# Halves after the next chunk's decays, decayed queries on VectorE, masks inside the clamp

## The chip, the cores and the metric

The kernel runs on one core of a Trainium2 chip. The metric is the device time of one execution in microseconds (us), the median of several runs. The engines are named as the profile names them: PE is TensorE (matmuls, with PEld for its weight loads), DVE is VectorE, ACT is ScalarE, POOL is GpSimd, SP is SyncE, whose queue issues all DMAs of this kernel. PE has two clock levels, 2.4 and 1.2 GHz; the profile gives the granted clock as a share of the higher one.

## The reference, cut to what matters

The model has two layers (1024 channels, 256 context tokens and 256 latent tokens). Each layer is a half-step feed-forward part, a token mixer and another feed-forward part. The token mixer runs three recurrences over the tokens in both directions and merges them: a gated delta rule (4 heads), retention (4 heads) and Mamba-2 SSD (16 heads in 2 groups). The last layer gives an output for the latent tokens alone.

The delta rule, in chunks, needs per head and direction a triangular matrix of key products with decays, and a matrix of query-key products with decays:

```python
diff = gc[..., :, None] - gc[..., None, :]
a_mat = (einsum('nbhik,nbhjk->nbhij', kc, kc)
         * where(strict, exp(where(strict, diff, 0.0)), 0.0) * bc[..., :, None])
sol = triangular_solve(eye(CHUNK) + a_mat, rhs, left_side=True, lower=True)
p_mat = (einsum('nbhik,nbhjk->nbhij', qc, kc)
         * where(incl, exp(where(incl, diff, 0.0)), 0.0))
```

The SSD scan (chunk_gla) has the same decays, and its part from the state is the query, decayed, times the state:

```python
intra = einsum('nbghij,nbghjv->nbghiv', scores[:, :, :, None] * dmat, vc)
o_c = einsum('bgik,bghkv->bghiv', xc[3], s) * xc[4][..., None]     # q s, times q_dec = exp(gc)
oc = (oc_f + flip(oc_b) + D * sx) * silu(s_z)
yc = rms_norm(oc per group, ssd_norm_g)
```

## The kernel before

All matmuls of weights are done as three passes of a split number: a value is cast to a shorter float (its high half) and the rest is the low half; L141 to L143 (mm3) multiply high by high, high by low and low by high. Each weight block (128x512) is loaded by SP's queue (raw, L110), cast on ACT (whi, L121) and subtracted on DVE or POOL (wlo, L123; pool_lo says which blocks go to POOL). Four blocks can be ahead of PE.

Every instruction is written in a program order, and a planner (the framework's scheduler, with its own costs) sets from that order and from what is ready in its model the order of each engine's queue. Queues then run strictly in that order. DMAs are in SP's queue, weight loads and others mixed.

The mixer (mix_main, L1424) runs the delta rule (gdn, L781) and lets a generator fill PE beside it: self.take(us) draws so many microseconds of projections (gdn_z, retention, ssd_project) from it. In layer 0 gdn runs twice with two heads and four output chunks of 128 tokens (och = 0 to 3); in layer 1 once with four heads, in two pairs, with output for chunks 2 and 3 alone. The preparation, L889 to L937, does for each pair of heads and each chunk c:

- L905: clamps on DVE. Rg holds the running sums of log decays as rows (loaded from DRAM by rows_in), G the same as columns. Slots 0 and 1 of E are min(Rg - G, 0) forward, slots 2 and 3 the same backward (only for output chunks), slots 4 and 5 are max(Rg - G, 0) backward. L908 and L909 take exp on ACT.
- L912, L915: key-key and key-query products on PE, into PSUM (ps).
- L917: kks, the key products times the strict upper mask triUs, on DVE. L920 and L921: M = kks * column * E. L923: M times the rows Rb on POOL.
- L928: kq = key-query products * column * mask (triU or triL), four on DVE. L930: PT = kq * E.
- L936, L937: the decayed queries Q of the delta rule (ACT, POOL).

Then the 32x32 diagonal blocks of M go to DRAM and back (L945, L952: d1, B), a substitution on DVE inverts them in 31 steps (L957, L959), merges of blocks make the inverse of the chunk, and the scan over chunks follows.

The SSD part (ssd, L1219) runs after the delta rule, per group g of 8 heads, with the merge (gates and branch projections) as PE's filling. prep(c, d) makes for chunk c and direction d the decays: Relu and exp on ACT (L1281, L1283) for E; and where a state comes in (c != d) exp of the rows R (L1287), times the queries BC (L1288: POOL in layer 0, DVE in layer 1). out(c) does the products (L1314), the gating (L1317), the mean of squares (L1319, L1323), the reciprocal root in eight small DVE instructions on 128x1 (tile snv, L1326, then rsqrt, L252 to L260), its broadcast by PE (L1330), the scaling (L1333), and last the halves of the chunk (L1336 cast on ACT to ysch, L1337 subtract on DVE to yscl), which the third branch of the merge reads. The loop at L1349 runs prep(next, 0), out(c), prep(next, 1).

Of the kernel before, what the change touches and what calls it, by code (L numbers as in the profile page):

```python
# [8 lines left out]
F32 = mybir.dt.float32  # L9
# [6 lines left out]
P = 128  # L16
# [30 lines left out]
class Net:  # L47
# [410 lines left out]

    def mix_setup(self, ctx):
        nc, io, cp = self.nc, self.io, self.cp  # L460
        self.masks = cp.tile([P, 3, P], F32, name="masks")
        nc.sync.dma_start(out=self.masks, in_=io["masks"])
        self.triU, self.triL, self.triUs = (self.masks[:, i, :] for i in range(3))
        self.prow = cp.tile([P, DEPTH, PR_N], F32, name="prow")
        nc.sync.dma_start(out=self.prow, in_=io["prow"].rearrange("(o l) n -> o l n", o=1).broadcast_to([P, DEPTH, PR_N]))
        self.rt = cp.tile([P, 4, 48], F32, name="rt_")
        nc.gpsimd.memset(self.rt, 0.0)

        for lo, hi in ((PC_GCW, PC_GNG), (PC_GNG, PC_N)):
            v = self.pcol[:, :, lo:hi]  # L470
            nc.vector.tensor_scalar(out=v, in0=v, scalar1=0.5, scalar2=None, op0=MUL)
# [309 lines left out]
    def gdn(self, H, gp, pool0, gtok):  # L781
# [105 lines left out]
        with ExitStack() as st:  # L887
            pp = st.enter_context(tc.tile_pool(name=f"gprep{tag}", bufs=1, side="right", reuse_waits="tile"))
            for p in range(0, nh, 2):  # L889
                Rg = pp.tile([P, 2, 2, T], F32, tag="Rg", name="Rg")  # L890
                Rb = pp.tile([P, 2, 2, T], F32, tag="Rb", name="Rb")
                for d in range(2):
                    self.rows_in(Rg[:, d], self.dR[d * 20 + h0 + p:d * 20 + h0 + p + 2, :])
                    self.rows_in(Rb[:, d], dB[d * nh + p:d * nh + p + 2, :])
                pair = lambda t, c: t[:, c].rearrange("p (d h) n -> p d h n", d=2)[:, :, p:p + 2]
                for c in range(4):
                    out = c in och
                    cs = ac(c)
                    E = pp.tile([P, 6, P], F32, tag="E", name="E", bufs=2)
                    for i in range(2):  # L900
                        for d, slot, op in ((0, i, MIN), (1, 2 + i, MIN), (1, 4 + i, MAX)):
                            if slot in (2, 3) and not out:
                                continue
                            g = h0 + p + i
                            nc.vector.tensor_scalar(out=E[:, slot], in0=Rg[:, d, i, cs], scalar1=self.G[:, c, d, g:g + 1],  # L905
                                                    scalar2=0.0, op0=SUB, op1=op)
                    ne = 4 if out else 2
                    nc.scalar.activation(out=fl(E[:, 0:ne]), in_=fl(E[:, 0:ne]), func=AF.Exp)  # L908
                    nc.scalar.activation(out=fl(E[:, 4:6]), in_=fl(E[:, 4:6]), func=AF.Exp, scale=-1.0)  # L909
                    ps = v4(self.mx("kk"))  # L910
                    for i in range(2):
                        nc.tensor.matmul(ps[:, i], kf[:, p + i, cs], kf[:, p + i, cs], start=True, stop=True)  # L912
                    if out:
                        for i in range(2):
                            nc.tensor.matmul(ps[:, 2 + i], kf[:, p + i, cs], qf[:, p + i, qc(c)], start=True, stop=True)  # L915
                    kks = pp.tile([P, 2, P], F32, tag="kks", name="kks", bufs=2)
                    nc.vector.tensor_tensor(out=kks, in0=ps[:, 0:2], in1=self.triUs.unsqueeze(1).to_broadcast([P, 2, P]), op=MUL)  # L917
                    for i in range(2):
                        q = p + i
                        nc.vector.scalar_tensor_tensor(out=M[:, c, q], in0=kks[:, i], scalar=rk[:, c, q:q + 1], in1=E[:, i], op0=MUL, op1=MUL)  # L920
                        nc.vector.scalar_tensor_tensor(out=M[:, c, nh + q], in0=kks[:, i], scalar=bb[:, c, q:q + 1], in1=E[:, 4 + i],  # L921
                                                       op0=MUL, op1=MUL)
                    nc.gpsimd.tensor_tensor(out=pair(M, c), in0=pair(M, c), in1=Rb[:, :, :, cs], op=MUL)  # L923
                    if out:
                        kq = pp.tile([P, 4, P], F32, tag="kq", name="kq", bufs=1)
                        for i in range(2):
                            for d, m in ((0, self.triU), (1, self.triL)):
                                nc.vector.scalar_tensor_tensor(out=kq[:, 2 * d + i], in0=ps[:, 2 + i], scalar=rk[:, c, p + i:p + i + 1],  # L928
                                                               in1=m, op0=MUL, op1=MUL)
                        nc.vector.tensor_tensor(out=pair(PT, c - n0), in0=kq.rearrange("p (d h) n -> p d h n", d=2),  # L930
                                                in1=E[:, 0:4].rearrange("p (d h) n -> p d h n", d=2), op=MUL)
                    self.take(wt[2])
                for d in range(2):
                    for i in range(2):
                        q_ = Q[:, d, p + i]
                        nc.scalar.activation(out=q_, in_=Rg[:, d, i, self.oc], func=AF.Exp)  # L936
                        nc.gpsimd.tensor_tensor(out=q_, in0=q_, in1=qf[:, p + i], op=MUL)  # L937
# [281 lines left out]
    def ssd(self):  # L1219
        nc, l, tc = self.nc, self.l, self.tc  # L1220
        och, oc = self.och, self.oc
        with ExitStack() as st:
            pool = st.enter_context(tc.tile_pool(name=f"ssd{l}", bufs=1, side="right", reuse_waits="tile"))
            for g in range(2):
# [18 lines left out]
                def state(n):  # L1243
                    for d in sorted(V):
# [7 lines left out]
                        else:  # L1252
# [5 lines left out]
                DI = pool.tile([P, 8, P], F32, tag="DI", name="DI")  # L1258
                nc.gpsimd.tensor_tensor(out=DI, in0=self.ident.unsqueeze(1).to_broadcast([P, 8, P]),
                                        in1=self.prow[:, l, PR_D + 8 * g:PR_D + 8 * g + 8].unsqueeze(2).to_broadcast([P, 8, P]), op=MUL)  # L1260
                units = {}

                def prep(c, d):

# [20 lines left out]
                    if c != d:  # L1285
                        rf = r.rearrange("p h t -> p (h t)")
                        nc.scalar.activation(out=rf, in_=rf, func=AF.Exp)  # L1287
                        (nc.vector if l else nc.gpsimd).tensor_tensor(out=r, in0=r, in1=self.BC[:, 2 + g, cs].unsqueeze(1).to_broadcast([P, 8, P]), op=MUL)  # L1288

                    nc.vector.tensor_tensor(out=e, in0=e, in1=gm[:, d].unsqueeze(1).to_broadcast([P, 8, P]), op=MUL)  # L1290
                    if d == 0:
# [9 lines left out]
                def out(c):  # L1301
# [29 lines left out]
                    for q in range(4):  # L1331
                        t = 4 * g + q
                        nc.vector.scalar_tensor_tensor(out=O[:, q], in0=O[:, q], scalar=self.pcol[:, l, PC_SNG + t:PC_SNG + t + 1],  # L1333
                                                       in1=rs, op0=MUL, op1=MUL)
                    yh, yl = (y[:, 4 * g:4 * g + 4, c * P - oc.start:(c + 1) * P - oc.start] for y in self.ysc)
                    nc.scalar.copy(out=yh, in_=O)  # L1336
                    nc.vector.tensor_tensor(out=yl, in0=O, in1=yh.bitcast(F32), op=SUB)  # L1337

                w = self.ssd_fill
                weighted(0)  # L1340
# [8 lines left out]
                for i, c in enumerate(och):  # L1349
# [4 lines left out]
                        yield w[3] * part  # L1354
                    if nxt is not None:
                        prep(nxt, 1)
                        yield w[4]


# [362 lines left out]
def constants():  # L1722

    i, j = np.arange(P)[:, None], np.arange(P)[None, :]
    m = np.zeros((P, 3, P), np.float32)
    m[:, 0] = i <= j
    m[:, 1] = i >= j
    m[:, 2] = i < j
    d = np.arange(384)[None, :] - P - np.arange(P)[:, None]
    dist = d.astype(np.float32)  # L1730
    n_freq = P // 4
# [72 lines left out]
```

## Time and profile before

| | |
|---|---|
| median of 3 runs | 2776.03 us (2774.65 to 2779.43) |
| the profiled execution | 2773.71 us |
| its span, first to last instruction | 2771.9 us |
| mean granted clock of PE | 0.978 |
| PE busy | 2602.5 us |
| DVE busy | 2088.3 us |
| ACT busy | 1213.0 us |
| POOL busy | 745.7 us |

Busy shares are means over stages with different limits. The delta rule lies at about 440 to 860 us (layer 0, two calls) and 2060 to 2360 us (layer 1), the SSD scan at about 860 to 1090 us and 2370 to 2510 us. A wait in the views is time in which an engine stood still before an instruction, with the instruction that ended last before it.

### The profile page before, as it was taken

Reading aid. Unit: us, or ns where it says so; the run is one execution under the profiler, and the core shown is the slowest. Engines: PE = TensorE matmul, PEld = TensorE weight load, DVE = VectorE, ACT = ScalarE, POOL = GpSimd, SP = SyncE. Lnnn points to the kernel's source line nnn. Section 1 sums busy time; section 2 is a strip of 40 time slices with the busy share of each in tenths; the row PEclk is TensorE's granted clock in tenths of the full one; section 3 lists DMA queues with packets and bytes.
Section 4 is the critical chain, followed back from the end, with each engine's and each line's share of the span. In section 5 each row is a group of like instructions: output and inputs, shape, how many; then the busy total and the mean of one; then the engine's idle time right before and its main releaser. Section 6 shows DMA issues by size and latency. Waiting matters only on the chain.

```text
span 2771.9 us, 45529 instructions
## 1 busy us (share of the span) xinstructions
PE 2602.5 (94%) x16136; PEld 2216.4 (80%) x16136; DVE 2088.3 (75%) x4122; ACT 1213.0 (44%) x2388; POOL 745.7 (27%) x627
## 2 busy tenths in 40 slices
PE   8999999899899999999999999999988889889998
PEld 6888887777777777888887888888877768778997
DVE  5888878868878585488987778854778885786666
ACT  3333256344345643363332543323655354554553
POOL 1000144422444454250000520002443433453100
PEclk9999999999999999999999999999999999999999
DMA  8566655423425455366665466643545333656665
GB/s 280 178 187 188 172 165 147 118 62 105 147 77 158 155 152 156 106 172 197 194 187 185 136 208 195 189 125 97 174 115 166 110 99 89 194 184 187 199 183 152
DMA packets 292808, 435.99 MB, mean 157 GB/s; under 512 B 42628, under 2 KB 109828, under 8 KB 292452
## 3 DMA queue, kind: packets, MB, share of 16 engines
q1 hardware_dynamic: 292580, 433.09, 53.1%
q8 instruction: 126, 2.06, 0.3%
q14 instruction: 102, 0.84, 0.1%
HBM read 401.86 MB, written 31.13 MB: 156 GB/s over the span
## 4 chain that ended last, share of the span: by engine, by line
PE 63%; DVE 19%; DMA 7%; issue 5%; ACT 3%; POOL 3%; SPq 1%; DVEq 0%; ACTq 0%; POOLq 0%
PE p L141 9%; PE p L143 9%; PE p L142 9%; DVE cacc L533 4%; DMA raw<-wst 4%; PE pd L141 3%; PE pd L143 3%; PE pd L142 3%; DVE wlo L123 3%; PE gate L141 1%; PE gate L143 1%; PE gate L142 1%; ACT whi L121 1%; PE br L141 1%; PE br L143 1%
## 5 line engine op out<-in xcount | busy, mean ns | idle before, releaser
L121 ACT CAST whi<-raw 128x512 fp32r<-128x512 f32 x1003 | 613.5, 617 | 819.5 <-PE pd L142 195.4
L123 DVE TENSOR_TENSOR wlo<-raw,whi 128x512 fp32r<-128x512 f32 x803 | 596.8, 746 | 233.3 <-ACT whi L121 226.5
L141 PE MATMUL p<-uh,whi 128*128 128x512 f32 (+1 forms) x1216 | 445.3, 366 | 1.8 <-ACT whi L121 1.8
L143 PE MATMUL p<-uh,wlo 128*128 128x512 f32 (+1 forms) x1216 | 440.2, 362 | 0.2 <-DVE wlo L123 0.2
L142 PE MATMUL p<-ul,whi 128*128 128x512 f32 (+1 forms) x1216 | 440.2, 362 | 0.0
L123 POOL TENSOR_TENSOR wlo<-raw,whi 128x512 fp32r<-128x512 f32 x200 | 288.5, 1445 | 484.5 <-ACT whi L121 467.6
L190 DVE SCALAR_TENSOR_TENSOR acc<-raw,cT,acc 128x512 f32<-128x512 f32 x448 | 320.5, 753 | 87.9 <-DMA raw<-wst 86.2
L307 POOL TENSOR_TENSOR y<-y,piv 128x256 f32<-128x256 f32 x30 | 27.6, 950 | 884.5 <-ACT piv L305 884.5
L141 PEld LDWEIGHTS p<-uh,whi 128*128 128x128 f32 x1216 | 229.0, 188 | 43.4 <-ACT whi L121 4.4
L143 PEld LDWEIGHTS p<-uh,wlo 128*128 128x128 f32 x1216 | 229.1, 188 | 37.3 <-DVE wlo L123 0.6
L142 PEld LDWEIGHTS p<-ul,whi 128*128 128x128 f32 x1216 | 229.2, 188 | 34.2
L141 PE MATMUL pd<-ach,whi 128*128 128x512 f32 (+1 forms) x660 | 232.0, 351 | 0.0
L143 PE MATMUL pd<-ach,wlo 128*128 128x512 f32 (+1 forms) x660 | 229.4, 348 | 0.0
L142 PE MATMUL pd<-acl,whi 128*128 128x512 f32 (+1 forms) x660 | 229.2, 347 | 0.0
L533 DVE SCALAR_TENSOR_TENSOR cacc<-craw,pcol,cacc 128x508 f32<-128x508 f32 (+2 forms) x192 | 169.4, 889 | 17.6 <-ACT cacc L528 16.0
L141 PEld LDWEIGHTS pd<-ach,whi 128*128 128x128 f32 x660 | 125.0, 189 | 17.4 <-ACT whi L121 1.4
L143 PEld LDWEIGHTS pd<-ach,wlo 128*128 128x128 f32 x660 | 125.0, 189 | 16.3 <-DVE wlo L123 0.5
L142 PEld LDWEIGHTS pd<-acl,whi 128*128 128x128 f32 x660 | 125.0, 189 | 15.2
L141 PE MATMUL gate<-uh,whi 128*128 128x512 f32 (+1 forms) x384 | 135.4, 353 | 0.0
L143 PE MATMUL gate<-uh,wlo 128*128 128x512 f32 (+1 forms) x384 | 130.9, 341 | 0.8 <-POOL wlo L123 0.8
L142 PE MATMUL gate<-ul,whi 128*128 128x512 f32 (+1 forms) x384 | 131.4, 342 | 0.0
L411 ACT CAST ach<-pr 128x512 fp32r<-128x512 f32 (+1 forms) x88 | 50.0, 568 | 164.8 <-DVE pr L410 164.8
(477 smaller groups left out, 6057.4 us busy)
## 6 DMA issues: line engine op xcount, KB each, us to landing
raw<-wst SPq DMA_DIRECT2D x1313, 256.0 KB, 2.8
R<-dR SPq DMA_DIRECT2D x24, 512.0 KB, 6.0
dah<-y SPq DMA_DIRECT2D x9, 1024.0 KB, 5.6
y<-dah SPq DMA_DIRECT2D x28, 256.0 KB, 5.1
Rg<-dR SPq DMA_DIRECT2D x8, 512.0 KB, 5.2
Rb<-dB SPq DMA_DIRECT2D x8, 512.0 KB, 4.6
dx<-xo SPq DMA_DIRECT2D x16, 256.0 KB, 2.9
xt<-dx SPq DMA_DIRECT2D x4, 1024.0 KB, 8.4
```

The lines of the kernel that those rows point to most:

```text
L121: nc.scalar.copy(out=hi, in_=r)
L123: e.tensor_tensor(out=lo, in0=r, in1=hi.bitcast(F32), op=SUB)
L141: nc.tensor.matmul(out, wh, xh, start=start, stop=False)
L142: nc.tensor.matmul(out, wh, xl, start=False, stop=False)
L143: nc.tensor.matmul(out, wl, xh, start=False, stop=stop)
L190: eng.scalar_tensor_tensor(out=acc, in0=r, scalar=c, in1=acc, op0=MUL, op1=ADD)
L307: (nc.gpsimd if m >= self.ln_dve[0] else nc.vector).tensor_tensor(out=y[:, m, c], in0=y[:, m, c], in1=piv, op=SUB)
L411: nc.scalar.copy(out=F["ach"][:, m], in_=pr[:, :n])
L533: nc.vector.scalar_tensor_tensor(out=a[:, :, lo:hi], in0=r[:, :, lo + d:hi + d], scalar=w[:, tap:tap + 1], in1=a[:, :, lo:hi], op0=MUL, op ...
```

## The change

There are three edits.

1. In the delta rule the masks move into the clamp. Two of the constant masks are now 0 inside the triangle and -30000 outside (minU, minL; the strict mask goes). A masked clamp is one scalar_tensor_tensor, min(Rg - G, mask), so that exp gives 0 outside. The third clamp, max(Rg - G, 0), becomes a Relu on ACT with the bias nG = -G, made once per head pair on DVE. kks and kq go: M and PT are made directly from the products in PSUM. The lower part of M is no longer zero, and what follows reads only its upper part.
2. In the scan, the multiply of the decayed queries (L1288) is on DVE in both layers.
3. The halves of a finished chunk are put aside in a list (done) and made by halves() after prep(next, 1), before the filling that follows it. For the last chunk of a group they come right after out, as before.

```diff
-        self.masks = cp.tile([P, 3, P], F32, name="masks")
+        self.masks = cp.tile([P, 4, P], F32, name="masks")
...
-        self.triU, self.triL, self.triUs = (self.masks[:, i, :] for i in range(3))
+        self.triU, self.triL, self.minU, self.minL = (self.masks[:, i, :] for i in range(4))
...
+                nG = pp.tile([P, 4, 2], F32, tag="nG", name="nG", bufs=2)
+                nc.vector.tensor_scalar(out=nG, in0=self.G[:, :, 1, h0 + p:h0 + p + 2], scalar1=-1.0, scalar2=None, op0=MUL)
...
-                        for d, slot, op in ((0, i, MIN), (1, 2 + i, MIN), (1, 4 + i, MAX)):
-                            if slot in (2, 3) and not out:
-                                continue
-                            g = h0 + p + i
-                            nc.vector.tensor_scalar(out=E[:, slot], in0=Rg[:, d, i, cs], scalar1=self.G[:, c, d, g:g + 1],
-                                                    scalar2=0.0, op0=SUB, op1=op)
+                        g = h0 + p + i
+                        for d, low in ((0, self.minU), (1, self.minL)):
+                            if d == 0 or out:
+                                nc.vector.scalar_tensor_tensor(out=E[:, 2 * d + i], in0=Rg[:, d, i, cs], scalar=self.G[:, c, d, g:g + 1],
+                                                               in1=low, op0=SUB, op1=MIN)
+                        nc.scalar.activation(out=E[:, 4 + i], in_=Rg[:, 1, i, cs], func=AF.Relu, bias=nG[:, c, i:i + 1])
...
-                    kks = pp.tile([P, 2, P], F32, tag="kks", name="kks", bufs=2)
-                    nc.vector.tensor_tensor(out=kks, in0=ps[:, 0:2], in1=self.triUs.unsqueeze(1).to_broadcast([P, 2, P]), op=MUL)
...
-                        nc.vector.scalar_tensor_tensor(out=M[:, c, q], in0=kks[:, i], scalar=rk[:, c, q:q + 1], in1=E[:, i], op0=MUL, op1=MUL)
-                        nc.vector.scalar_tensor_tensor(out=M[:, c, nh + q], in0=kks[:, i], scalar=bb[:, c, q:q + 1], in1=E[:, 4 + i],
+                        nc.vector.scalar_tensor_tensor(out=M[:, c, q], in0=ps[:, i], scalar=rk[:, c, q:q + 1], in1=E[:, i], op0=MUL, op1=MUL)
+                        nc.vector.scalar_tensor_tensor(out=M[:, c, nh + q], in0=ps[:, i], scalar=bb[:, c, q:q + 1], in1=E[:, 4 + i],
                                                        op0=MUL, op1=MUL)
...
-                        kq = pp.tile([P, 4, P], F32, tag="kq", name="kq", bufs=1)
                         for i in range(2):
-                            for d, m in ((0, self.triU), (1, self.triL)):
-                                nc.vector.scalar_tensor_tensor(out=kq[:, 2 * d + i], in0=ps[:, 2 + i], scalar=rk[:, c, p + i:p + i + 1],
-                                                               in1=m, op0=MUL, op1=MUL)
-                        nc.vector.tensor_tensor(out=pair(PT, c - n0), in0=kq.rearrange("p (d h) n -> p d h n", d=2),
-                                                in1=E[:, 0:4].rearrange("p (d h) n -> p d h n", d=2), op=MUL)
+                            for d in range(2):
+                                nc.vector.scalar_tensor_tensor(out=PT[:, c - n0, d * nh + p + i], in0=ps[:, 2 + i], scalar=rk[:, c, p + i:p + i + 1],
+                                                               in1=E[:, 2 * d + i], op0=MUL, op1=MUL)
...
-                        (nc.vector if l else nc.gpsimd).tensor_tensor(out=r, in0=r, in1=self.BC[:, 2 + g, cs].unsqueeze(1).to_broadcast([P, 8, P]), op=MUL)
+                        nc.vector.tensor_tensor(out=r, in0=r, in1=self.BC[:, 2 + g, cs].unsqueeze(1).to_broadcast([P, 8, P]), op=MUL)
...
-                    nc.scalar.copy(out=yh, in_=O)
-                    nc.vector.tensor_tensor(out=yl, in0=O, in1=yh.bitcast(F32), op=SUB)
+                    done.append((c, O))
+
+                def halves():
+
+                    while done:
+                        c, O = done.pop()
+                        yh, yl = (y[:, 4 * g:4 * g + 4, c * P - oc.start:(c + 1) * P - oc.start] for y in self.ysc)
+                        nc.scalar.copy(out=yh, in_=O)
+                        nc.vector.tensor_tensor(out=yl, in0=O, in1=yh.bitcast(F32), op=SUB)
...
                     if nxt is not None:
                         prep(nxt, 1)
+                    halves()
+                    if nxt is not None:
                         yield w[4]
...
-    m = np.zeros((P, 3, P), np.float32)
+    m = np.zeros((P, 4, P), np.float32)
     m[:, 0] = i <= j
     m[:, 1] = i >= j
-    m[:, 2] = i < j
+    m[:, 2:] = (m[:, :2] - 1) * np.float32(30000.0)
```

## Rows read from the trace of the kernel before

**Rows 1.** The page's first part: busy us of each engine, share, instructions

```profile
PE 2602.5 (94%) x16136; PEld 2216.4 (80%) x16136; DVE 2088.3 (75%) x4122; ACT 1213.0 (44%) x2388; POOL 745.7 (27%) x627
```

**Rows 2.** Waits of PE, whole span: total us, times, longest us

```profile
PE str L1181 <- DVE BC L536: 12.8, 2, 7.0
...
PE rsc L653 <- DVE pt L657: 6.7, 1, 6.7
PE rof L686 <- DVE on L680: 6.2, 4, 2.5
...
PE rsc L653 <- DVE pt L660: 5.2, 3, 4.0
```

**Rows 3.** Waits of PE from 850 to 1085 us

```profile
PE sv L1330 <- DVE snv L260: 15.9, 3, 6.3
```

**Rows 4.** Timeline of DVE: start, us, instruction, idle before and its releaser

```profile
533.28 0.18 DVE L957 TENSOR_TENSOR tm<-B,X 64x31 f32<-64x31 f32 x1 [7.28 <-DMA B<-d]
...
735.46 0.18 DVE L957 TENSOR_TENSOR tm<-B,X 64x31 f32<-64x31 f32 x1 [8.11 <-DMA B<-d]
```

**Rows 5.** Windows: us, busy PE, PEld, DVE, ACT, POOL, granted clock, DMA, GB/s

```profile
755.00:760.00 5.00, 5.00 (x15) 4.04 (x14) 4.63 (x10) 0.59 (x1) 0.00 (x0) 0.50 0.30 98
...
2160.00:2170.00 10.00, 7.15 (x47) 5.91 (x46) 10.00 (x38) 4.36 (x10) 3.23 (x3) 1.00 0.31 96
```

**Rows 6.** Groups of DVE instructions, 486 to 521 us: busy us, mean ns

```profile
L905 DVE TENSOR_SCALAR E<-Rg,G 128x128 f32<-128x128 f32 x24 | 10.0, 464 | 2.1 <-DMA Rg<-dR 2.1
L930 DVE TENSOR_TENSOR PT<-kq,E 128x512 f32<-128x512 f32 x4 | 5.7, 1427 | 0.0
L928 DVE SCALAR_TENSOR_TENSOR kq<-kk,col,masks 128x128 f32<-128x128 f32 x16 | 4.8, 340 | 0.0
L920 DVE SCALAR_TENSOR_TENSOR M<-kks,col,E 128x128 f32<-128x128 f32 x8 | 3.8, 475 | 0.0
L921 DVE SCALAR_TENSOR_TENSOR M<-kks,col,E 128x128 f32<-128x128 f32 x8 | 3.8, 474 | 0.0
...
L917 DVE TENSOR_TENSOR kks<-kk,masks 128x256 f32<-128x256 f32 x4 | 1.7, 415 | 0.7 <-PE kk L915 0.7
```

**Rows 7.** Timeline of DVE, 707 to 712 us

```profile
707.54 1.11 DVE L928 SCALAR_TENSOR_TENSOR kq<-kk,col,masks 128x128 f32<-128x128 f32 x4
...
710.70 1.26 DVE L905 TENSOR_SCALAR E<-Rg,G 128x128 f32<-128x128 f32 x6
```

**Rows 8.** Source views of seven instructions: count, least/median/greatest ns, starts

```profile
L905 DVE TENSOR_SCALAR E<-Rg,G x88: 271/277/1382, 488.2 to 2166.2; 128x128 f32<-128x128 f32 x88
L920 DVE SCALAR_TENSOR_TENSOR M<-kks,col,E x32: 335/346/1397, 496.7 to 2168.5; 128x128 f32<-128x128 f32 x32
L928 DVE SCALAR_TENSOR_TENSOR kq<-kk,col,masks x48: 331/339/347, 489.7 to 2170.2; 128x128 f32<-128x128 f32 x48
L1281 ACT ACTIVATE E<-R,G x192: 383/388/405, 872.8 to 2479.1; 128x128 f32<-128x128 f32 x192
L1288 POOL TENSOR_TENSOR R<-R,BC x12: 2340/2459/3362, 884.9 to 1069.7; 128x1024 f32<-128x1024 f32 x12
L1288 DVE TENSOR_TENSOR R<-R,BC x8: 1210/1222/1955, 2386.3 to 2482.3; 128x1024 f32<-128x1024 f32 x8
L1337 DVE TENSOR_TENSOR yscl<-O,ysch x12: 684/958/2470, 909.1 to 2503.9; 128x512 fp32r<-128x512 f32 x12
```

**Rows 9.** Timeline of DVE, 975 to 978 us

```profile
975.26 0.16 DVE L259 SCALAR_TENSOR_TENSOR snv<-snv 128x1 f32<-128x1 f32 x1
975.46 2.32 DVE L260 SCALAR_TENSOR_TENSOR snv<-snv 128x1 f32<-128x1 f32 x1
```

**Rows 10.** Timeline of POOL in the same stretch

```profile
975.42 2.34 POOL L1288 TENSOR_TENSOR R<-R,BC 128x1024 f32<-128x1024 f32 x1 [0.21 <-ACT R L1287]
```

**Rows 11.** Timeline of SP's queue: the last transfer of M's blocks

```profile
524.14 0.42 SPq L945 DMA_DIRECT2D d<-M  x1
```

**Rows 12.** Source view of L936: what its engine waited for, us, times

```profile
  DMA Rg<-dR: 9.8, 6
```

More of the change, by code (lines that the diff above doesn't have):

```diff
@@ L1260, in ssd @@
                                         in1=self.prow[:, l, PR_D + 8 * g:PR_D + 8 * g + 8].unsqueeze(2).to_broadcast([P, 8, P]), op=MUL)
-                units = {}
+                units, done = {}, []
                 def prep(c, d):
@@ L1334, in out @@
                                                        in1=rs, op0=MUL, op1=MUL)
-                    yh, yl = (y[:, 4 * g:4 * g + 4, c * P - oc.start:(c + 1) * P - oc.start] for y in self.ysc)
-                    nc.scalar.copy(out=yh, in_=O)
-                    nc.vector.tensor_tensor(out=yl, in0=O, in1=yh.bitcast(F32), op=SUB)
+                    done.append((c, O))
[5 more added lines that the diff above has]
+                        nc.vector.tensor_tensor(out=yl, in0=O, in1=yh.bitcast(F32), op=SUB)
                 w = self.ssd_fill
```

## The prediction

> **What bounds the kernel now.** I read the engine shares first: TensorE (PE) is busy 94% of the span and VectorE (DVE) 75% [rows 1], so the span is PE's work plus the stretches in which PE stands still or runs at the lower clock. I asked next what PE waits for [rows 2, 3] and looked up in the timelines where that happens. The waits that this change can touch are in two places.
>
> In the delta rule, PE waits 6.7 us for a retention product (pt, L657), 7.0 us for a convolved tile (BC, L536; 12.8 us in two waits, so the other, in layer 1, is 5.8 us), and 5.2 and 6.2 us for pt (L660) and on (L680) [rows 2]. In the two layer-0 cases DVE's queue has reached the block substitution (L957) and stands there until the blocks B have come back from DRAM, at 533.28 and 735.46 us, after 7.28 and 8.11 us idle [rows 4]; what PE needs is behind that. In layer 1 DVE is simply full: busy 10.00 of 10 us while PE is busy 7.15 [rows 5]. So in both layers the preparation of the masked matrices, nearly all DVE work, is late.
>
> In the scan of layer 0, PE waits 15.9 us in three waits for the small reciprocal-root chain (L252 to L260, tile snv) [rows 3]. After a long wait PE also runs slower: from 755 to 760 us it is busy all 5.00 us at a granted clock of 0.50, the 1.2 GHz level, which costs 2.5 us more [rows 5].
>
> **The delta rule's preparation.** Four chunks of a head pair in layer 0 are 24 clamps, 4 kks, 16 M, 16 kq and 4 PT [rows 6]. By count times mean: 24x0.464 + 4x0.415 + 8x0.475 + 8x0.474 + 16x0.340 + 4x1.427 = 31.5 us. Neighbours overlap by 0.08 us (six clamps take 1.26 us, one alone 0.277, so one every 0.197 [rows 7, 8]); 64 such overlaps are 5.1 us, so DVE is held 26.4 us.
>
> Much of that is not work. Clamps and M, which read only SBUF, run from 0.27 and 0.34 us to 1.38 and 1.40 us, while kq, of M's form and shape but with one input from PSUM, never took more than 347 ns in 48 [rows 8]: one kq follows another every 0.257 us ((1.11 - 0.34)/3) [rows 7, 8]. The long ones stand beside GpSimd (POOL) work, as in [rows 9, 10].
>
> After the change the 16 M and 16 PT have exactly kq's form: 32x0.257 = 8.2 us. The 16 masked clamps aren't in the trace; they have two SBUF inputs as M has, so 0.257 each without blocking, 4.1 us, plus 16/24 of the clamps' present excess, 24x(0.464 - 0.277) = 4.5, so 3.0 us (bounds 0 and 16x1.1). Sum 15.3 us: 11 us of DVE less per four output chunks, of which about 10 before the last M. nG is one small instruction per head pair, at the 0.16 us of the chain's [rows 9]: nothing.
>
> How much of the 10 us does B gain? The four transfers of M's blocks share SP's queue with the weight loads; the last was issued at 524.14 us [rows 11]. It can stay there (gain 0), or the stalls of 6.7 and 7.0 us can go whole. I take 4 us each, nearer the upper end because DVE was idle only after the last M. In layer 1, four output chunks save 4x2.8 and four without output about 1 each (0.6 from fewer instructions: 4x0.197 + 0.33 against 2x0.257, the rest from unblocked M), some 15 us if blocking is as dense as in layer 0; I take 11. PE's waits there are 5.2 + 6.2 + 5.8 = 17.2 us (upper end; lower end 0): 6, half of what DVE saves. The slow-clock tail shrinks with its wait: 1.5 of the 2.5 us. Together 4 + 4 + 6 + 1.5 = 15.5 us.
>
> What it adds: 32 Relus on ScalarE (ACT), 0.388 us by the same instruction in the scan [rows 8], 12.4 us in all. ACT is busy 4.36 of 10 us there [rows 5], so that work hides. The wait that they add does not surely hide: each first Relu of a pair waits for the DMA of Rg, and behind it in ACT's queue are the weight casts (whi), for which PE waits. The existing Q exponentials stand in that same wait for 9.8 us in six waits [rows 12] without a large PE stall, so I charge 1 us for each of four loads, 4 us (bounds 0 and 9.8, as much again as those waits).
>
> **Decayed queries on DVE in layer 0.** 12 multiplies leave POOL, 12x2.459 = 29.5 us, and 12x1.222 = 14.7 us come to DVE [rows 8]. In the second of the three waits, the last chain instruction took 2.32 us instead of 0.16 while POOL's multiply ran from 975.42 for 2.34 us [rows 9, 10]; if that is so in all three, 3x2.2 = 6.5 us go. Against it: the multiply of a chunk's forward direction is earlier in the program than the chain of the chunk before and can now stand ahead of it on DVE, 1.22 us; twice, 2.4 us. Net 4 us, with 1 us of clock: 5. Bounds: all 15.9 us gained, or the loss of rival 3.
>
> The Trainium skill, "SBUF — State Buffer", section "Who interferes with whom", has a rule that speaks against this edit: a DVE instruction with two SBUF inputs and a GpSimd instruction that reads SBUF exclude each other, whichever starts first keeping the ports to its end. By that rule each new DVE multiply could hold one of POOL's weight splits up to 1.2 us, 14.7 us of POOL in all, half of the 29.5 us that the edit takes off POOL; no run before the change shows that direction priced, and the sum stays.
>
> **Halves behind the next chunk's backward decays.** 8 of the 12 cast-and-subtract pairs move (a chunk with a successor: 3x2 in layer 0, 1x2 in layer 1). DVE's one takes 0.958 us [rows 8]. Nobody reads the halves until the third branch of the merge, after the scan, so nothing waits for them. DVE no longer stands for the cast behind decay work, but PE was fed in those moments. No DMA moves. I take 0; bounds: 1 us each side per moved pair (a subtract less, or more, ahead of a chain), 8 us.
>
> **Sum.** 15.5 + 5 - 4 = 16.5 us, from the profiled execution's 2773.7 (span 2771.9 plus 1.8): 2757.2. The median of the timed runs is 2.3 us above that execution, so 2759.5, say 2760.
>
> **Rivals.** 1. *The transfers hold B.* M is early but its four transfers stay behind the same weight loads in SP's queue, so both layer-0 stalls and the tail stay. For it: the 524.14 us issue [rows 11]. Against: the order of the queues is planned from the program anew, and M is earlier there too. 16.5 - 9.5 = 7 us gain: 2769. 2. *All of it goes.* DVE was the only late one: 6.7 + 7.0 + 17.2 + 15.9 = 46.8 us of waits less 4 us for ACT: 2733. Against: port blocking by POOL's weight splits stays, and DVE's substitution stays as long. 3. *The scan's DVE queue becomes the late one, slower than before.* In the chunks with a successor (6 in layer 0) both multiplies, 2x1.22 us, get in ahead of the chain that PE waits for, and each wait draws a slow-clock tail of up to 2.5 us: 6x4.9 = 29.6 us, less the 6.5 us of port stalls gone: +23, and with half of the delta rule's gain, -8, about +15: 2791. It decides if the chain starts more than one multiply (1.22 us) later than now in most chunks. Against: DVE had idle time in this stretch and the chain has the earlier place in the program than the backward multiply. 4. *Nothing to measure.* The preparation is faster but the saved waits come back where PE next meets DVE (the convolutions behind the substitution), and the Relu waits eat the rest: 2774.
>
> **How the numbers follow.** Forecast (2745 to 2768) 0.52; rival 1 0.17; rival 2 0.07; rival 3 0.11; rival 4 0.13. No change is what lies within 0.2%, 5.5 us, about what a measurement of this kernel can tell: 2770.5 to 2781.6. Of rival 1, 2769, I count 0.12 as faster and 0.05 as no change. Faster 0.52 + 0.12 + 0.07 = 0.71, same 0.18, slower 0.11. The range for 8 in 10 leaves out rivals 2 and 3 at most: 2743 to 2777; the forecast's own is 2745 to 2768.
>
> **What the profile after would show.** Right: M and PT at most 0.35 us on DVE; the substitution's first instruction some 4 us earlier against the start of its preparation; the waits for pt (L657) and BC halved; the three waits for snv down from 15.9 to about 10 or less; no POOL multiply in the scan. Wrong: M still blocked with a PSUM input; B's arrival unmoved though the last M is earlier; ACT waiting for Rg with PE waiting for whi behind it; waits for snv or for R (the decayed queries) in layer 0 longer than before.

## The result, and the profile after

The changed kernel took 2746.57 us in the median (2739.34 to 2749.3) beside 2777.73 us for the kernel before: ratio 0.9885, 95% interval 0.9859 to 0.9910. Beside other kernels later it gave 0.9916 (0.9902 to 0.9930). The forecast was 2760.

```profile
PE 2594.9 (94%) x16136; PEld 2214.7 (81%) x16136; DVE 2068.4 (75%) x4078; ACT 1224.9 (45%) x2420; POOL 719.8 (26%) x615
```

Against [rows 1] PE lost 7.6 us of busy time for the same number of instructions. Where the span went is seen in four stretches, bounded by the same PE instructions in both kernels: from the first small projection (sm) of a layer to the scan's first state product (sS), and from there to the scan's last sv. The edits shift the line numbers: in the changed kernel the clamps are L907, M L922 and L923, PT L929, the substitution starts at L956, and the multiply of the decayed queries is L1287. First the windows of the kernel before: layer 0 up to the scan, its scan, layer 1 up to the scan, its scan (columns as in [rows 5]).

```profile
417.10:865.50 448.40, 409.24 (x2497) 335.38 (x2496) 356.10 (x836) 202.27 (x394) 170.01 (x149) 0.97 0.39 112
865.50:1086.30 220.80, 203.00 (x1207) 163.24 (x1206) 158.06 (x232) 118.41 (x252) 112.11 (x63) 0.96 0.52 151
1994.20:2370.00 375.80, 329.53 (x2427) 289.26 (x2425) 292.48 (x662) 187.72 (x389) 138.49 (x112) 0.96 0.43 126
2370.00:2501.70 131.70, 112.67 (x941) 100.97 (x941) 102.24 (x157) 76.62 (x165) 71.28 (x47) 0.95 0.62 182
```

And of the changed kernel:

```profile
419.50:859.60 440.10, 406.72 (x2496) 335.23 (x2495) 347.68 (x806) 207.97 (x411) 167.59 (x149) 0.98 0.39 114
859.60:1063.20 203.60, 198.12 (x1207) 160.13 (x1207) 154.44 (x244) 118.84 (x252) 84.04 (x51) 0.99 0.56 163
1970.60:2343.80 373.20, 326.37 (x2412) 286.86 (x2411) 285.78 (x633) 192.08 (x403) 140.11 (x112) 0.96 0.44 125
2343.80:2475.00 131.20, 112.22 (x956) 100.72 (x956) 104.83 (x159) 76.63 (x165) 71.91 (x47) 0.96 0.64 186
```

The delta-rule stretch of layer 0 is 8.3 us shorter, the scan of layer 0 17.2, the delta-rule stretch of layer 1 2.6, its scan 0.5. That is 28.6 us, while the whole span is 24.4 shorter; the parts that the change does not touch took 4.2 us more in this profile. In the scan of layer 0, PE's idle time fell from 17.8 to 5.5 us (length less busy time) and its busy time by 4.9 for the same 1207 instructions, while the granted clock rose from 0.96 to 0.99: 12.3 us of waits and 4.9 of slow clock. In layer 1 the idle time did not fall (46.3 and 46.8), and the two stretches there do not hold the same work: 15 PE instructions fewer stand before the scan (x2427, x2412) and 15 more in it (x941, x956). By the names of their tiles 14 of them are products of the merge's gates, which stand at 0.23 us each in the timeline: some 3 us, as much as that stretch is shorter.

The waits of PE that answer to [rows 2], whole span, and to [rows 3], the scan of layer 0 (pt L661 answers to pt L660 before, pt L658 to L657):

```profile
PE str L1180 <- DVE BC L537: 9.9, 2, 5.6
...
PE rof L687 <- DVE on L681: 7.5, 4, 3.1
...
PE rsc L654 <- DVE pt L661: 5.2, 1, 5.2
...
PE rsc L654 <- DVE pt L658: 4.5, 1, 4.5
```

```profile
PE sv L1329 <- DVE snv L260: 4.5, 3, 2.7
```

The substitution's first instructions in layer 0, as [rows 4], and the groups of the first preparation, as [rows 6]:

```profile
532.20 0.18 DVE L956 TENSOR_TENSOR tm<-B,X 64x31 f32<-64x31 f32 x1 [5.59 <-DMA B<-d]
...
729.47 0.18 DVE L956 TENSOR_TENSOR tm<-B,X 64x31 f32<-64x31 f32 x1 [3.59 <-DMA B<-d]
```

```profile
L907 DVE SCALAR_TENSOR_TENSOR E<-Rg,G,masks 128x128 f32<-128x128 f32 x16 | 13.4, 891 | 3.3 <-DMA Rg<-dR 3.3
L929 DVE SCALAR_TENSOR_TENSOR PT<-kk,col,E 128x128 f32<-128x128 f32 x16 | 4.5, 341 | 0.0
L922 DVE SCALAR_TENSOR_TENSOR M<-kk,col,E 128x128 f32<-128x128 f32 x8 | 2.7, 344 | 0.2 <-ACT E L911 0.2
```

M (L923 is the same, 342 ns) and PT now cost what kq cost. The masked clamps cost 0.89 us each in this first preparation, 0.755 in the mean of all 56.

### The profile page after: what moved, and what is told of

Same layout as the page of the kernel before. It is cut to its first block, busy times and chain, and to the rows that moved or that the text cites. A ratio compares the mean times of both kernels' runs of the same rounds, so it can differ in the third digit from the quotient of the medians.

```text
span 2747.5 us, 45507 instructions
## 1 busy us (share of the span) xinstructions
PE 2594.9 (94%) x16136; PEld 2214.7 (81%) x16136; DVE 2068.4 (75%) x4078; ACT 1224.9 (45%) x2420; POOL 719.8 (26%) x615
## 5 line engine op out<-in xcount | busy, mean ns | idle before, releaser
L123 DVE TENSOR_TENSOR wlo<-raw,whi 128x512 fp32r<-128x512 f32 x803 | 586.8, 733 | 256.9 <-ACT whi L121 249.8
L141 PEld LDWEIGHTS p<-uh,whi 128*128 128x128 f32 x1216 | 229.1, 188 | 42.9 <-ACT whi L121 5.0
```

Source lines behind the costliest of these rows:

```text
L123: e.tensor_tensor(out=lo, in0=r, in1=hi.bitcast(F32), op=SUB)
L141: nc.tensor.matmul(out, wh, xh, start=start, stop=False)
```

## The experiments

Lengths in us of the four stretches in each profile, and the ratio of the timed runs to the kernel before. Kernels that share the code of a stretch show how far one profile can be off.

| kernel | layer 0 to scan | scan 0 | layer 1 to scan | scan 1 | ratio, 95% interval |
|---|---|---|---|---|---|
| before | 448.4 | 220.8 | 375.8 | 131.7 | 1 |
| changed | 440.1 | 203.6 | 373.2 | 131.2 | 0.9885 (0.9859 to 0.9910) |
| changed, again (e12) | 442.6 | 202.3 | 376.1 | 128.3 | 0.9916 (0.9902 to 0.9930) |
| e1 queries on DVE only | 448.4 | 203.7 | 375.3 | 131.1 | 0.9949 (0.9931 to 0.9967) |
| e2 halves only | 450.0 | 216.1 | 377.0 | 131.7 | 0.9993 (0.9978 to 1.0008) |
| e3 delta rule only | 439.8 | 216.7 | 372.8 | 133.9 | 0.9953 (0.9935 to 0.9970) |
| e4 plain clamps | 442.0 | 203.6 | 371.6 | 133.5 | 0.9917 (0.9897 to 0.9937) |
| e5 POOL pass added | 440.6 | 219.1 | 375.0 | 130.4 | 0.9965 (0.9952 to 0.9977) |
| e6 third clamp on DVE | 446.5 | 204.7 | 366.6 | 132.2 | 0.9908 (0.9892 to 0.9925) |
| e7 less fill in preparation | 448.8 | 201.9 | 372.5 | 139.7 | 0.9955 (0.9941 to 0.9968) |
| e8 diagonal on DVE | 442.7 | 201.3 | 373.3 | 132.1 | 0.9905 (0.9889 to 0.9920) |
| e9 Relus in layer 0 only | 441.2 | 203.4 | 366.5 | 132.3 | 0.9905 (0.9890 to 0.9920) |
| e10 e9, diagonal on DVE in layer 0 | 438.5 | 203.2 | 370.2 | 132.5 | 0.9902 (0.9886 to 0.9917) |
| e11 halves as before | 439.3 | 203.8 | 369.8 | 132.4 | 0.9926 (0.9913 to 0.9940) |

**One part at a time (e1, e2, e3).** On the kernel before, e1 makes one line of the change, e2 the hunks with `done` and `halves()`, e3 all the others.

```diff
-                        (nc.vector if l else nc.gpsimd).tensor_tensor(out=r, in0=r, in1=self.BC[:, 2 + g, cs].unsqueeze(1).to_broadcast([P, 8, P]), op=MUL)
+                        nc.vector.tensor_tensor(out=r, in0=r, in1=self.BC[:, 2 + g, cs].unsqueeze(1).to_broadcast([P, 8, P]), op=MUL)
```

> Only the decayed queries' multiply goes to DVE in layer 0; the delta rule's preparation and the halves stay as before. Theory A (ports): the 17 us by which the changed kernel's scan of layer 0 is shorter (220.9 to 203.6 us) come from POOL's 2.4 us multiplies, which held single DVE instructions of the chain behind sv and of the work just ahead of it. Then this kernel alone has them: scan of layer 0 at 204 to 207 us, waits of PE for snv there down from 15.9 to about 5 us, total 2777.7 - 16 = about 2762. Theory B (the halves uncover the chain): scan of layer 0 stays at 216 us or more, waits for snv 12 us or more, total above 2771. Theory C (the scan is entered in another order by the faster delta rule): as B, no gain here.

> Only the cast-and-subtract pair of a finished chunk is moved behind the next chunk's backward decays. Theory A: nothing waits for the halves, so the total is within 4 us of before (2774 to 2782) and PE's waits for snv in layer 0 stay between 13 and 18 us. Theory B: the pair stood ahead of work that PE waits for; scan of layer 0 shorter by 10 us or more, total about 2767.

> Only the delta rule's preparation is changed (masks in the clamps, third clamp on ACT, M and PT from PSUM); scan as before. In the changed kernel the stretch up to the scan is 8.2 us shorter in layer 0 and 2.6 us in layer 1. Theory A: that is this part's own, so 2777.7 - 11 = about 2767, with the scan of layer 0 at 219 to 223 us. Theory B (the scan's gain hangs on the delta rule's order): total about 2755, scan of layer 0 near 204 us. Theory C (the delta part's gain in layer 0 is only where the weights happened to fall): total within 5 us of before.

Theory A held in all three. The queries alone give the whole of the shorter scan (203.7 us) and 5.1 thousandths of the time, 14 us. PE's waits in that scan, e1:

```profile
PE sv L1330 <- DVE snv L260: 5.0, 3, 2.7
```

The delta rule alone gives 13 us. The halves alone give 0.7 thousandths, with an interval over no change. The scan with the multiply on POOL was 216.1 and 216.7 us in e2 and e3 for 220.8 before, and PE's waits for snv in it 12.7 and 12.6 for 15.9, a little under what theory A allowed both; so one profile of that scan is good to 5 us, and some of the 17.2 was that. The 203.7 of e1 lies just under the 204 of its theory.

**POOL given back its instruction (e5).**

```diff
+                        if l == 0:
+                            nc.gpsimd.tensor_tensor(out=r, in0=r, in1=self.zero4[:, 0:1].unsqueeze(2).to_broadcast([P, 8, P]), op=ADD)
```

> The changed kernel, and behind DVE's multiply of the decayed queries in layer 0 GpSimd adds a column of zeros to them (128x1024, two SBUF inputs, in place): POOL is given back an instruction of the size that the change took off it, and DVE's own instructions stay. Theory A (a POOL instruction of 2.4 us holds the DVE instruction beside it until it ends): the scan of layer 0 goes back from 203.6 us to 214 to 221, single snv instructions of 1 to 2.4 us come back, total 10 to 17 us over the changed kernel, 2757 to 2764. Theory B (the gain is another order on DVE, with the products ready earlier): the queries are ready later but PE did not wait for them before either; scan of layer 0 at 203 to 207 us, total 2745 to 2751.

Theory A: 219.1 us, and a ratio 8 thousandths over the changed kernel's first (22 us, more than the theory's 17), 5 over its second (14 us). PE's waits in that scan:

```profile
PE sv L1331 <- DVE snv L260: 11.2, 4, 4.6
PE sv L1324 <- ACT szl L1320: 2.8, 1, 2.8
PE sO L1315 <- POOL R L1289: 1.2, 1, 1.2
```

The waits for snv are back at 11.2 us for 4.5. The pass also makes the queries themselves later, theory B, and PE waited 1.2 us for them. The timelines of DVE and of POOL in one of the waits of e5 (start, us, instruction):

```profile
1034.83 0.15 DVE L1327 TENSOR_SCALAR snv<-sv 128x1 f32<-128x1 f32 x1
1035.02 0.15 DVE L252 TENSOR_SCALAR snv<-snv 128x1 int32<-128x1 int32 x1
1035.20 1.70 DVE L254 TENSOR_TENSOR snv<-snv 128x1 f32<-128x1 f32 x1
1036.93 1.18 DVE L255 SCALAR_TENSOR_TENSOR snv<-snv 128x1 f32<-128x1 f32 x1
```

```profile
1034.99 1.89 POOL L1289 TENSOR_TENSOR R<-R,zero 128x1024 f32<-128x1024 f32 x1 [1.16 <-DVE snv L1327]
1036.84 1.26 POOL L123 TENSOR_TENSOR wlo<-raw,whi 128x512 fp32r<-128x512 f32 x1
```

L254 ends at 1036.90, when POOL's pass ends (1036.88); L255 at 1038.11, when POOL's split ends (1038.10). Work on a single column waits for the rest of a POOL instruction, twice in one chain.

**The masked clamps (e4).** This kernel leaves the causal mask out.

```diff
-                                nc.vector.scalar_tensor_tensor(out=E[:, 2 * d + i], in0=Rg[:, d, i, cs], scalar=self.G[:, c, d, g:g + 1],
-                                                               in1=low, op0=SUB, op1=MIN)
+                                nc.vector.tensor_scalar(out=E[:, 2 * d + i], in0=Rg[:, d, i, cs], scalar1=self.G[:, c, d, g:g + 1],
+                                                        scalar2=0.0, op0=SUB, op1=MIN)
```

> The changed kernel with its masked clamps in the old form with one tensor input and no mask: the causal mask is left out of the computation. In the changed kernel a masked clamp took 0.755 us in the mean (56 of them), 0.34 where no POOL instruction ran beside it; the old form took 0.426. Theory A (the preparation is as long as DVE's own work): DVE's own time in each preparation falls by 4 to 7 us, the blocks B are back as much earlier, and the total is 6 to 12 us under the changed kernel, 2735 to 2741. Theory B (PE's fill work between two chunks sets the pace of the preparation, or the transfers that of B): the preparation stays within 2 us as long, and the total within 4 us of the changed kernel's 2747.

Theory B on the time: the ratio is the changed kernel's second, and the preparations, from the first clamp to the end of the last M, took 25.2, 23.8 and 64.8 us for 26.4, 22.8 and 65.2. E, M and PT took 18.5, 21.7 and 24.2 us of DVE in the three preparations, for 21.8, 21.2 and 27.4, less of a gain than theory A named too. The plain clamps were held as well where a POOL instruction was running as they began, 25 of 26, for 28 of 30 masked ones in the changed kernel; of its 64 M's, with their PSUM input, 10 began beside POOL and none was held (counted from the traces; held is over 1.3 times the usual 0.28 or 0.34 us).

```profile
L907 DVE TENSOR_SCALAR E<-Rg,G x56: 272/283/1385, 487.9 to 2126.3; 128x128 f32<-128x128 f32 x56
```

**What sets the preparation's pace (e7).**

```diff
-self.gdn_fill = ((2, 4, 5, 18, 1, 1, 3, 4), (2, 4, 5, 20, 0.5, 0.35, 3, 4))[self.outs[0]]
+self.gdn_fill = ((2, 4, 3, 26, 1, 1, 3, 4), (2, 4, 3, 36, 0.5, 0.35, 3, 4))[self.outs[0]]
```

> The changed kernel with 3 instead of 5 us of PE's fill work handed out behind each chunk of the delta rule's preparation, and what is taken off there (2 us for each of 4 chunks twice in layer 0, and of 8 in layer 1) added to the substitution. Theory A (PE's fill work in program order sets the pace of the preparation, not DVE): from the first clamp to the last M 65 us become about 49 in layer 1, and 26.4 and 22.8 about 18 to 20 in layer 0. Theory B (DVE's own work sets it, 20 to 27 us of the preparation plus the rest that it does there): at most 4 us shorter in any of them. The total follows only if B is what PE waits for: by A up to 8 us under the changed kernel; if the waits just move into the substitution, within 4 us of 2747.

Theory A in layer 1, by the length of the preparation. The M's there in the changed kernel, then clamps and M's of e7 (the starts of first and last):

```profile
L923 DVE SCALAR_TENSOR_TENSOR M<-kk,col,E x16: 335/341/351, 2085.9 to 2141.0; 128x128 f32<-128x128 f32 x16
```

```profile
L907 DVE SCALAR_TENSOR_TENSOR E<-Rg,G,masks x24: 337/344/1372, 2082.7 to 2123.2; 128x128 f32<-128x128 f32 x24
L923 DVE SCALAR_TENSOR_TENSOR M<-kk,col,E x16: 336/340/344, 2095.0 to 2127.7; 128x128 f32<-128x128 f32 x16
```

From the first clamp (2076.2 in the changed kernel, 2082.7 here) to the end of the last M, 65 us become 45, by 8 times 2 us of fill and a little more; before the change they were 66. In layer 0 26.4 us became 22.3 and 22.8 became 22.3, less than theory A said and nearer to theory B.

The fill has a PE part and a DVE part, and e7 takes both out: in the preparation of layer 1 PE was busy 54.0 us in the changed kernel and 39.1 here, DVE 57.6 and 38.8. So e7 does not tell PE's fill work from the DVE work that goes with it. What is shown is that the fill, and not the clamps, M and PT, sets that length: DVE was busy 65.0 of 65.8 us there before the change and 57.6 of 65.2 after.

The time got worse all the same. The bounds of the four stretches cut the work at other places here (41 PE instructions fewer before the scan of layer 1, 43 more in it), so the two stretches of a layer are taken together: 650.7 us in layer 0 for 643.7 in the changed kernel, and 512.2 in layer 1 for 504.4. A preparation that is 20 us shorter, with the fill handed out later, bought nothing. Waits behind it grew, on from 7.5 to 16.2 us and in layer 0 the merge's blocks (XX) from 3.4 to 9.8; why they grew is not shown.

**Where the third clamp belongs, and what the rest of POOL costs (e6, e8, e9, e10).** e6 makes the first edit, e9 makes it in layer 1 alone; e8 makes the second, e10 makes it in layer 0 alone, on top of e9.

```diff
-                        nc.scalar.activation(out=E[:, 4 + i], in_=Rg[:, 1, i, cs], func=AF.Relu, bias=nG[:, c, i:i + 1])
+                        nc.vector.tensor_scalar(out=E[:, 4 + i], in0=Rg[:, 1, i, cs], scalar1=self.G[:, c, 1, g:g + 1],
+                                                scalar2=0.0, op0=SUB, op1=MAX)
```

```diff
-                        nc.gpsimd.tensor_tensor(out=e, in0=e, in1=DI, op=ADD)
+                        nc.vector.tensor_tensor(out=e, in0=e, in1=DI, op=ADD)
```

> The changed kernel with the third clamp (subtract, maximum with 0) back on DVE in the old form, 32 instructions, in place of the 32 Relus on ACT. The prediction charged the Relus 4 us, for the wait for Rg with the weight casts behind them. Theory A (that charge is right): DVE is held 32 x 0.2 to 0.4 us longer, which is off the path, and ACT goes free: total 2 to 4 us under the changed kernel, 2743 to 2745. Theory B (the Relus cost nothing and save DVE time that sets the end): total 3 to 8 us over it, 2750 to 2755, with B back 1 to 2 us later in each layer-0 preparation. Theory C (neither end is on the path): within 2 us of 2747.

> The changed kernel with the diagonal's addition (E + DI, 128x1024, 2.43 us on POOL, 8 in layer 0 and 4 in layer 1) on DVE too, the same step as the change made for the decayed queries. Theory A (POOL's long instructions still hold DVE's short ones): the snv instructions keep no stall over 1.5 us, scan of layer 0 3 to 6 us under 203.6, scan of layer 1 1 to 4 us under 131.2, total 2738 to 2743. Theory B (DVE, busy 80% of the scan of layer 1, takes 1.2 us more for each and is now itself late): scan of layer 1 3 us or more longer, layer 0 no shorter than 202, total 2747 to 2754.

> The changed kernel with the third clamp on ACT in layer 0 and back on DVE in layer 1. With it on DVE in both layers the stretch up to the scan was 446.5 us in layer 0 (changed kernel 440.2) and 366.6 us in layer 1 (373.2), while kernels with the same code there differed by 3 us at most. Theory A (the Relus pay in layer 0, where DVE is late, and cost in layer 1, where the preparation goes at the pace of PE's fill work and ACT's queue has the weight casts): 439 to 443 us in layer 0 and 365 to 369 in layer 1, total 4 to 8 us under the changed kernel. Theory B (the two differences were chance): layer 1 again at 371 to 375 us and the total within 3 us of the changed kernel.

> The kernel with the third clamp on ACT in layer 0 alone, and in layer 0 also the diagonal's addition on DVE (8 of 2.43 us leave POOL). With that in both layers the scan of layer 0 was 201.3 us (changed kernel 203.6) and that of layer 1 132.1 (131.2). Theory A (POOL's blocks still cost a little in layer 0): scan of layer 0 at 200 to 202 us, total 2 to 3 us under the kernel without that step. Theory B (no block that PE waits for is left): scan of layer 0 at 203 to 205 us, total within 2 us of it.

Of the totals of e6 and e8 to e10 none can be told from the changed kernel's second ratio, 0.9916: neither a better version nor a worse one is shown. By the stretches, the Relus on ACT are worth some 6 us in layer 0 (446.5 in e6, one profile, for 438.5 to 442.7 in the eight other kernels with Relus and masked clamps there, e7 aside). So each of e6's theories has part of it. In layer 1 the third clamp on DVE gave 366.6, 366.5 and 370.2, with the Relus 369.8 to 376.1 in six kernels; with the scan behind it, which evens out where the gates' products fall, 498.8, 498.8 and 502.7 for 502.2 to 506.7: likely a cost of some 5 us, but the two sets touch, and e9's total is only 3 us under e12's. Theory A of e9 is not settled. The diagonal on DVE gave 201.3 and 203.2 for 202.3 to 204.7: no theory A of e8 or e10, and no harm in layer 1 either. Yet DVE was held less: what its instructions in the scan of layer 0 took over the shortest of their form (counted from 0.15 us on) was 50.3 us before the change, 34.4 after it and 24.4 in e8. PE's waits for snv there are 4.5 us in the changed kernel and 4.1 in e8: the 10 us of holding that e8 takes away lay where PE did not wait.

**The other side of the halves (e11), and the measure (e12).**

> The changed kernel with the cast-and-subtract pair back at the end of its chunk, as before. Theory A (nothing waits for the halves): scan of layer 0 at 202 to 206 us, of layer 1 at 130 to 133, total within 3 us of the changed kernel. Theory B (the pair stood ahead of work on DVE that PE waits for; alone the move gave 2 us and a scan of layer 0 at 216.1 us for 220.9): scan of layer 0 at 207 us or more, total 4 us or more over the changed kernel.

> The changed kernel once more, beside the three others on one chip, as their measure. Every theory expects what it gave: ratio 0.986 to 0.991, scan of layer 0 at 203 to 205 us, the stretch up to it 439 to 443 us, and that of layer 1 at 372 to 375.

Edit of e11: the hunks with `done` and `halves()` undone. Its scans are as long as with the halves moved, theory A. Its ratio is 1.0 thousandth over e12's, 3 us, inside the intervals; e2's was 0.7 under 1. Together: 0 to 3 us. e12 itself came out 3 thousandths over the first measurement, a little past the interval of that; I count with both.

## Why the prediction was right, and where it was not

Means over the profiles with the same code: layer 0 up to the scan 448.9 us before (3 profiles), 440.6 after (8): 8.3. Scan of layer 0 217.9 (before, e2, e3) and 203.6 (7 with the multiply on DVE and the diagonal on POOL, e7 aside): 14.3. Layer 1 up to the scan 376.0 (3) and 373.4 (6): 2.6; with its scan 507.5 and 504.8: 2.8. Sum 25.2 us (2.6 taken for layer 1), between the two measured 31 and 23; forecast 16.5.

The first median, 2746.57, lies 1.6 us inside the forecast's own range, 2745 to 2768. That it lies inside is in part luck, since misses of both signs stand behind it: against the forecast the scan brought 9.3 us more, the charge of 4 for the Relus did not show, the delta rule of layer 0 brought 1.2 less and that of layer 1 3.4 less.

**The scan was mis-sized: 5 us forecast, 14.3 measured.** The mechanism was right (e1, e5), the size was not, and it is the term that missed most. I had looked at the end of the chain, one stall of 2.2 us [rows 9, 10]. The timelines of DVE and of POOL before the change, in the run-up to that same wait and in it:

```profile
968.29 2.24 DVE L1240 TENSOR_TENSOR V<-xt,wv 128x512 f32<-128x512 f32 x1 [5.15 <-DMA xt<-dx]
...
973.98 1.25 DVE L258 TENSOR_TENSOR snv<-snv 128x1 f32<-128x1 f32 x1
```

```profile
967.59 2.40 POOL L1288 TENSOR_TENSOR R<-R,BC 128x1024 f32<-128x1024 f32 x1 [0.62 <-ACT R L1287]
973.94 1.27 POOL L123 TENSOR_TENSOR wlo<-raw,whi 128x512 fp32r<-128x512 f32 x1 [3.96 <-ACT whi L121]
```

And the same place in the changed kernel, DVE and POOL:

```profile
955.67 1.22 DVE L1287 TENSOR_TENSOR R<-R,BC 128x1024 f32<-128x1024 f32 x1 [3.08 <-ACT R L1286]
...
961.33 0.16 DVE L258 TENSOR_TENSOR snv<-snv 128x1 f32<-128x1 f32 x1
961.53 0.16 DVE L259 SCALAR_TENSOR_TENSOR snv<-snv 128x1 f32<-128x1 f32 x1
961.72 0.16 DVE L260 SCALAR_TENSOR_TENSOR snv<-snv 128x1 f32<-128x1 f32 x1
```

```profile
953.80 1.29 POOL L123 TENSOR_TENSOR wlo<-raw,whi 128x512 fp32r<-128x512 f32 x1 [6.70 <-ACT whi L121]
962.36 1.28 POOL L123 TENSOR_TENSOR wlo<-raw,whi 128x512 fp32r<-128x512 f32 x1 [7.27 <-ACT whi L121]
```

Three DVE instructions were held before, not one: V by 1.56 us (2.24 for 0.68, what another took), L258 by 1.09, L260 by 2.16, 4.8 us in all; POOL's split at 973.94 is one of the three, and it too is at another place now. The wait went from 6.31 to 0.97 us, the three together from 15.9 to 4.5. The prediction asked whether the other two waits hold such a stall: they did, DVE and POOL before the change.

```profile
920.35 1.94 DVE L254 TENSOR_TENSOR snv<-snv 128x1 f32<-128x1 f32 x1
...
1044.65 2.26 DVE L257 SCALAR_TENSOR_TENSOR snv<-snv 128x1 f32<-128x1 f32 x1
```

```profile
919.75 2.52 POOL L1288 TENSOR_TENSOR R<-R,BC 128x1024 f32<-128x1024 f32 x1 [2.19 <-ACT R L1287]
...
1044.56 2.34 POOL L1288 TENSOR_TENSOR R<-R,BC 128x1024 f32<-128x1024 f32 x1
```

Of the 2.4 us that I took off for the multiply standing ahead of the chain, at most half came. In the second wait the multiply starts at 955.67, after 3.08 us in which DVE was idle, and costs nothing. In the first it stands, with three other DVE instructions, between the end of the sum of squares (910.23) and the chain, which starts at 914.17; that is the longest wait left, 2.68 us. PE, then DVE, after the change:

```profile
909.28 0.95 PE L1322 MATMUL sv<-onesd,szl 128*128 128x1 f32 x8
```

```profile
912.43 1.21 DVE L1287 TENSOR_TENSOR R<-R,BC 128x1024 f32<-128x1024 f32 x1
...
914.17 0.14 DVE L1325 TENSOR_SCALAR snv<-sv 128x1 f32<-128x1 f32 x1
```

And the clock gave back 4.9 us, not 1 (4.8 in the means of the same profiles, beside 9.5 us of waits).

The rule of the Trainium skill, "SBUF — State Buffer", section "Who interferes with whom", holds in both directions. What it threatened, POOL's splits held by the new DVE multiplies, is seen in the groups of POOL in this scan, before and after:

```profile
L123 POOL TENSOR_TENSOR wlo<-raw,whi 128x512 fp32r<-128x512 f32 x26 | 36.7, 1415 | 47.5 <-ACT whi L121 44.9 <-PE gate L142 2.6
```

```profile
L123 POOL TENSOR_TENSOR wlo<-raw,whi 128x512 fp32r<-128x512 f32 x26 | 38.7, 1490 | 72.7 <-ACT whi L121 72.7
```

26 x 75 ns is 2 us of POOL, of the 14.7 that it could have been. Three of the 26 splits began while a new multiply ran (885.54, 1006.52 and 1023.10 us) and took 1.60 to 1.93 us for the usual 1.27, together 1.5 us. The prediction called that direction unpriced, but the trace before shows it: 6 of the 26 splits took 1.73 to 2.28 us there.

**The delta rule in layer 0 was right in sum, by errors that cancel.** B came earlier in each call as forecast (from the first clamp to the first instruction of the substitution, 45.1 to 40.9 us and 42.9 to 36.8; in e12 41.9 and 38.4), and 8.3 us came of it, in the means 6.5 of waits and 1.8 of PE's busy time, for 9.5 forecast. But DVE's work shrank by half of the 11 us: E, M and PT with kks and kq took 27.1 and 26.8 us, and 21.8 and 21.2 after, not 15.3; up to the last M 3.7 us went, not 10. The term of the clamps' blocking, 3.0 us, failed: 16 clamps cost 13.4 us, not 7.1. Six of them go at POOL's pace, as DVE and POOL show from 506 us:

```profile
506.76 6.23 DVE L907 SCALAR_TENSOR_TENSOR E<-Rg,G,masks 128x128 f32<-128x128 f32 x6
```

```profile
506.05 2.65 POOL L936 TENSOR_TENSOR Q<-Q,qf 128x512 f32<-128x512 f32 x2
508.67 1.33 POOL L925 TENSOR_TENSOR M<-M,Rb 128x512 f32<-128x512 f32 x1
509.96 2.89 POOL L123 TENSOR_TENSOR wlo<-raw,whi 128x512 fp32r<-128x512 f32 x2
```

M was held too before [rows 8]; now it never is, and the clamps are held more, mean 0.89 us for 0.464 [rows 6]. The second error: I passed on 4 of 10 us to B, and all of the 3.7 us that were saved got there, with a little more. The third: not all of that reached PE at the two waits that I named. The one for pt fell from 6.7 to 4.5 us, the one for BC from 7.0 to 4.3, and to 6.3 in e12; the other waits of the stretch gave the rest. Rival 1, the transfers hold B, is out.

**Layer 1 failed.** I took 6 us off the waits for pt (L660), on and BC, 17.2 us, from 11 us less work on DVE. DVE's own work did fall by 11 (38.7 to 27.4 us), and the waits are 18.3 us (5.2 + 7.5 + 5.6). The step that failed is that a full DVE makes the preparation late: it was full (65.0 of 65.8 us), the change freed 7 us of it, and the preparation still takes 65, 45 only with less fill (e7). Even then the layer was no shorter. The 2.6 us of the stretch are no proof of a gain, since some 3 us of the gates' products moved out of it behind the bound; over both stretches 2.8 us are left, and no wait is shown to have given them. Whether the Relus take some of the gain there is open (e9).

**The charge of 4 us for ACT's wait for Rg** had the wrong place. ACT stood 2.0 us before the Relus for Rg, in two waits, and PE's waits for whi over the whole span are 13.2 us before and 13.6 after. In layer 0 it is a gain of some 6 us (e6); in layer 1 it may be a cost of some 5 us.

**The halves at nothing** held: no scan tells them apart.

**What was to be seen after.** M and PT at most 0.35 us: yes (335 to 352 ns). The substitution 4 us earlier: 4.2 and 6.1. pt (L657) and BC halved: no, 6.7 to 4.5 and 12.8 to 9.9. The snv waits to 10 or less: 4.5. No POOL multiply in the scan: none.

## What to carry to other kernels

Where a chain of short DVE instructions is what PE waits for, look at every DVE instruction from the last PE result to the chain's end for one that is many times its unblocked length, and at what POOL runs then; price a POOL instruction by the DVE work that it holds in that chain, not by POOL's idle time. Holding that PE does not wait for costs nothing (e8). Moving such an instruction to DVE at half its length can cost DVE nothing: here DVE took 12 multiplies more (14.7 us) in that scan and was busy 3.6 us less. Work taken off an engine shortens a stage only where that engine sets its pace: find the other pace-maker (here the fill per chunk) before counting the saving, and see whether PE waits for what then comes earlier: in e7 the shorter preparation bought no time.

## What the runs showed of the hardware

A DVE clamp with one tensor input in SBUF waits for POOL as one with two does: 25 of 26 and 28 of 30 that began beside a running POOL instruction were held, up to 1.4 us. That agrees with the same section of the Trainium skill, which counts `tensor_scalar` among those that can contend; the masks' second input was not what got them held. With one input from PSUM none of 64 M's was held, though 10 began beside POOL. Six clamps in a row beside POOL took 6.23 us, where one follows another every 0.26 us without it.
